# A two-layer conv-attention trunk on one core: partial sums of the last weight matrix placed beside another stage, stores issued later, pools that wait tile by tile

## The chip, the cores and the metric

The kernel runs on 1 core of one Trainium2 chip. The metric is the device time of one execution in microseconds (us), lower is better. The five engines are called PE (TensorE, with PEld for its weight loads), DVE (VectorE), ACT (ScalarE), POOL (GpSimd) and SP (SyncE). SP does no arithmetic here: it issues every DMA of the kernel, one after the other, and a DMA that has to wait for a semaphore holds all that stand behind it.

## What is computed

Sequence 1024, width 1024, two layers in fp32. Layer 0 is a conformer convolution and a gated feed-forward (FFN, 2816 hidden). Layer 1 is causal differential attention (8 heads) and a second FFN:

```python
h = rms_norm(x, norm_g[l, 0]) * (1.0 + sc_m) + sh_m
y = conformer_conv(...) if l < N_CONV_LAYERS else diff_attention(h, k_shared, v_shared, ...)
x = x + g_m * rms_norm(y, norm_g[l, 1])
h = rms_norm(x, norm_g[l, 2]) * (1.0 + sc_f) + sh_f
y = conv_ffn(h, ffn_w_in[l], ffn_dw[l], ffn_dwb[l], ffn_w_out[l])
x = x + g_f * rms_norm(y, norm_g[l, 3])
```

with `conv_ffn(h) = (silu(g) * v) @ w_out`, where `g, v = split(causal_dwconv(h @ w_in))`.

## The kernel before, in words

Every matrix product is made exact enough by splitting each fp32 operand into a high and a low part: ACT copies the high part (`whi`, `wh`), POOL or DVE subtracts (`wlo`, `wl`), and PE makes three products for each. Weights come as 512 KB `raw` tiles (three buffers) through `wsplit`; `plan['pool']` says which share of the low parts POOL makes. The 1024 tokens go through the first part of the program (pools of `front`) in two halves of 512:

1. convolution of both halves, FFN of layer 0 on the first half, `qkv(0)`: Q, K, V of the first half (about 860 to 990 us);
2. FFN of layer 0 on the second half (`ffn(0, 1, ...)`), with three generators handed out beside its 60 steps by `interleave`: attention of the first half (`attn`, 48 steps), rows of the modulation (`gate_row`, `mod_scale`, `mod_col`), and `front_sums` (about 990 to 1445 us);
3. `wo_pre`, the residual and `wo_half` of the first half (to about 1565 us);
4. `qkv(1)`: Q, K, V of the second half, with the transposes of the first half's output beside V (to about 1706 us). Results go to DRAM (`qd`, `kd`, `vd`, `hfd`); `front.close()` ends the pools.
5. attention of the second half (about 1706 to 1965 us), with pools `back`, `ab` and four in PSUM. Its 37 steps (32 tiles of 128 queries, 4 to a head, and a tail) are written out by hand under `tc.manual_schedule()`: the instructions of each engine, SP's DMAs too, keep the order of the text. Beside each step stand a unit of the last FFN's first two products (`First.unit`, `one_more`) and two ticks of `sums_s`.
6. `wo` of the second half (pools `op`, `bp`), and the last FFN on all 1024 tokens, whose two products are made with 7 block products instead of 8.

Outside stage 5 the order on an engine is the framework's: it takes the text's order as a priority and places an instruction as soon as what it needs is there and, for a tile, a buffer is free.

The 7-product form needs sums of weight blocks. `sums_t(j, u, v)` (11 of them, line 933) loads two 512 KB tiles of `w_out`, makes four subtractions of 128x512 on POOL (line 940) and stores both tiles to `ftd` (lines 942, 943), which stage 6 reads. `sums_s(q, x, y, s)` (22 of them, line 945) does the like for `w_in`: two loads, four POOL operations (lines 951 to 957) and three stores to `sxd`, `syd`, `s1d` (lines 958 to 960), 1.25 MB. `front_sums` (line 962) makes all 11 `sums_t` and then `sums_s` for q = 10 to 21 in stage 2, with two `p4` buffers and one `p2`; q = 0 to 9 are made in stage 5.

In stage 5 a step's DMAs stand in this order: `load_kq` of the next head (lines 1141 to 1144, at step 1 of a head), `load_v` (line 1151, at step 0), the store of an attention result `o` (line 1227, every second step), the store of a unit's result `X` to `fdx` (line 1110), the next `rx` (line 1072), and the ticks of `sums_s`. Each store is issued where its data is made. The tag `q` of `back` (13 buffers of 4 KB) holds K, Q, `rx`, `ry` and `X`.

```python
def unit(self, mk):
    ...
    A.copy(self.x[:, (1 - i) * 512:(2 - i) * 512], ps)
    if i == 1:
        dma(out=fdx[q], in_=self.x)
```

Of the kernel before, what the change touches and what calls it, by code (L numbers as in the profile page):

```python
# [12 lines left out]
F32 = mybir.dt.float32  # L13
# [59 lines left out]
NWS, NSS, NQ, NHS = 12, 6, 13, 40  # L73
LA = 5
LAT = 4
QS = 10


# [28 lines left out]
def drain(g):  # L107
    for _ in g:
        pass
# [3 lines left out]
def trunk(ctx: ExitStack, tc: tile.TileContext, x, mw, cols, grow, w1, w2, wk, wv, wq, wo, win, wout, relb, onehot, lamr, out):  # L113
# [18 lines left out]
    def nm(s):  # L132
        uid[0] += 1
        return f"{s}_{uid[0]}"
# [10 lines left out]
    def pbank(pool, tag, name=None):  # L145
        return pool.tile([P, 512], F32, tag=tag, name=nm(name or "P" + tag))
# [556 lines left out]
    def qkv(half, hq, hkv, also_q=iter(()), also_v=iter(())):  # L703
        def stored(ps, scale, dst):
            hl = big.tile([P, 1024], F32R, tag="yf", bufs=4, name=nm("hl"))
            hi, lo = hl[:, 0:512], hl[:, 512:1024]
            if scale is None:
                A.copy(hi, ps)
                V.tensor_tensor(out=lo, in0=ps, in1=hi.bitcast(F32), op=ALU.subtract)
            else:  # L710
                A.activation(hi, ps, AF.Copy, scale=scale)
                V.scalar_tensor_tensor(out=lo, in0=ps, scalar=scale, in1=hi.bitcast(F32), op0=ALU.mult, op1=ALU.subtract)
            dma(out=dst, in_=hl.bitcast(F32).rearrange("p (l t) -> p l t", l=2))

        for h in range(NH):
            next(also_q, None)
            ps = pbank(pu, "u")
            featmm(ps, [wsplit(wq[h])], hq)
            stored(ps, 0.125, qd[h][half])
        for h in range(NH):  # L720
            ps = pbank(pu, "u")
            featmm(ps, [wsplit(wk[h])], hkv)
            stored(ps, None, kd[h][:, :, half * 512:(half + 1) * 512])

        def evac(t, nh, ps):
            sl = slice(nh * 512, (nh + 1) * 512)
            stored(ps, None, vd[half][t][:, :, sl])
        for nh in range(2):
            for _ in tokmm(hkv, lambda nh, pr: wv[nh, pr], nh, evac):
                next(also_v, None)  # L730
        drain(also_v)

    def two_heads(xn):

# [195 lines left out]

        return t.rearrange("p (k two j) -> p two k j", two=2, j=P)

    def sums_t(j, u, v):

        dma(out=u, in_=wout[1, 0, j])
        dma(out=v, in_=wout[1, 1, j])
        yield
        u0, u1, v0, v1 = u[:, 0:512], u[:, 512:1024], v[:, 0:512], v[:, 512:1024]
        for o, a, b in ((u0, v0, u0), (v0, v1, v0), (v1, v1, u0), (u1, u1, v1)):
            G.tensor_tensor(out=o, in0=a, in1=b, op=ALU.subtract)  # L940
            yield
        dma(out=ftd[j][0], in_=u)
        dma(out=ftd[j][1], in_=v)

    def sums_s(q, x, y, s):

        dma(out=y, in_=win[1, q + FC])
        yield
        (x0, x1), (y0, y1) = [[blocks(t)[:, i] for i in range(2)] for t in (x, y)]
        s_ = s.rearrange("p (k j) -> p k j", j=P)  # L950
        G.tensor_tensor(out=s_, in0=y0, in1=y1, op=ALU.add)
        yield
        G.tensor_tensor(out=y0, in0=x0, in1=y0, op=ALU.subtract)
        yield
        G.tensor_tensor(out=x0, in0=s_, in1=x0, op=ALU.subtract)
        yield
        G.tensor_tensor(out=x1, in0=x1, in1=x0, op=ALU.subtract)
        dma(out=sxd[q], in_=x)
        dma(out=syd[q], in_=y)
        dma(out=s1d[q], in_=s)  # L960
        yield

    def front_sums():
        def p4():
            return pre_.tile([P, 1024], F32, tag="p4", bufs=2, name=nm("p4"))
        for j in range(FC // 2):
            yield from sums_t(j, p4(), p4())
        for q in range(QS, FC):
            x = p4()
            dma(out=x, in_=win[1, q])  # L970
            yield from sums_s(q, x, p4(), pre_.tile([P, 512], F32, tag="p2", bufs=1, name=nm("p2")))

    pre_ = front.enter_context(tc.tile_pool(name="pre", bufs=1))
    gd_m1, gd_f1 = [dr.tile([1, D], F32, name=f"gdrow{n}") for n in range(2)]
# [4 lines left out]
    f = ffn(0, 1, hB, yB, gn_f0, ssB)  # L979
    interleave(itertools.islice(f, 60), (attn(at, 0, ssqA), NAT, 0, AE),  # L980
               (chain(gate_row(1, 2, 1, gn_m1, gd_m1), mod_scale(1, 4, 2, s_f1), mod_col(1, 3, sh_f1),
                       gate_row(1, 5, 3, None, gd_f1)), 32, 0, 60), (front_sums(), 5 * (FC // 2) + 6 * (FC - QS), 0, 60))
    ynA = wo_norm(ssqA)
    actA = []
    alongside(f, wo_pre(0, ynA, gpair, actA))
    xnB = residual(yB, ssB, 1, lambda t: xd[0][t], lambda t: xd[1][t])
    trB, hqB, hkvB = two_heads(xnB)
    xnA = wo_half(0, actA, gn_m1, trB)
    hA = []
    hfd = [dr.tile([P, D], F32, name=f"hfd{j}") for j in range(4)]  # L990
    qkv(1, hqB, hkvB, also_v=transposing(xnA, [hA], (hpair, s_f1, sh_f1), keep=hfd))
    front.close()


    back = ctx.enter_context(tc.tile_pool(name="back", bufs=1))
    att = ExitStack()
    ab = att.enter_context(tc.tile_pool(name="ab", bufs=1))
    psc = att.enter_context(tc.tile_pool(name="psc", bufs=2, space=PSUM))
    ptr = att.enter_context(tc.tile_pool(name="ptr", bufs=1, space=PSUM))
    pav = att.enter_context(tc.tile_pool(name="pav", bufs=1, space=PSUM))  # L1000
    pf = att.enter_context(tc.tile_pool(name="pf", bufs=1, space=PSUM))
    opool, bpool = [None], [None]

    def b2k(name="s"):
# [2 lines left out]
    def b4k(name="q", dt=F32):  # L1007
        return back.tile([P, 1024], dt, tag="q", bufs=NQ, name=nm(name))
# [56 lines left out]
    class First:  # L1065
# [20 lines left out]
        def sums(self, q):  # L1086

            x = self.raws.pop(q)
            if q < QS:
                yield from sums_s(q, x, b4k("ry"), b2k("S"))  # L1090

        def unit(self, mk):

            q, i = divmod(self.u, 2)
            self.u += 1
            if q >= FC:
                return
            if i == 0:
                self.ps, self.x = mk(), b4k("X")
            hi, lo = self.pairs.pop((q, i))  # L1100
            ps = self.ps
            for j in range(4):
                ah, al = H[1 + i][j]
                w, v = hi[:, j * P:(j + 1) * P], lo[:, j * P:(j + 1) * P]
                T.matmul(ps, lhsT=w, rhs=ah, start=(i == 0 and j == 0), stop=False, skip_group_check=True)
                T.matmul(ps, lhsT=w, rhs=al, start=False, stop=False, skip_group_check=True)
                T.matmul(ps, lhsT=v, rhs=ah, start=False, stop=(j == 3), skip_group_check=True)
            A.copy(self.x[:, (1 - i) * 512:(2 - i) * 512], ps)
            if i == 1:
                dma(out=fdx[q], in_=self.x)  # L1110

    first = First()
    bg = []

    def tick(n=1):
        for _ in range(n):
# [98 lines left out]
    def values(h, pr):  # L1215

        ah, al = AV[pr]
        nkb = NT + 2 * pr + 2
        po = pav.tile([P, 512], F32, tag="av", name=nm("Pav"))
        Vh = VV[h]  # L1220
        for kb in range(nkb):
            T.matmul(po[:, 0:256], lhsT=Vh[0][:, kb, :], rhs=ah[:, kb, :], start=(kb == 0), stop=False, skip_group_check=True)
            T.matmul(po[:, 0:256], lhsT=Vh[0][:, kb, :], rhs=al[:, kb, :], start=False, stop=False, skip_group_check=True)
            T.matmul(po[:, 0:256], lhsT=Vh[1][:, kb, :], rhs=ah[:, kb, :], start=False, stop=(kb == nkb - 1), skip_group_check=True)
        o = b2k("o")
        A.copy(o[:, 0:256], po[:, 0:256])
        dma(out=od[h][1][:, pr * 256:(pr + 1) * 256], in_=o[:, 0:256])
        sq = b2k("sq")
        A.activation(sq[:, 0:256], po[:, 0:256], AF.Square)
        return po, sq  # L1230
# [35 lines left out]
    for i in range(NTL + 5):  # L1266
        if i % NT == 1 and i // NT + 1 < NH:
            load_kq(i // NT + 1)
        if i % NT == 0 and i < NTL:
            load_v(i // NT)  # L1270
        if i < NTL:
            maxima(i)
        if 0 <= i - 2 < NTL:
            turned(i - 2)
        if i < NTL:
            exps(i)
        if i + 1 < NTL:
            scores(i + 1, 0)
            scores(i + 1, 1)
        t = i - 3  # L1280
        if i % 2 == 0 and 0 <= t < NTL:
            pairs[t] = values(t // NT, (t % NT) // 2)
        if t - 1 in pairs:
            squares(*pairs[t - 1])
        more(i)
        if 0 <= i - 2 < NTL:
            turned_lo(i - 2)
        if 0 <= i - 1 < NTL:
            difference(i - 1)
        if t - 1 in pairs:  # L1290
            V.tensor_copy(ss[:, t - 2:t], pairs.pop(t - 1)[0][:, 256:258])


    v = bsm(NTL)
    V.scalar_tensor_tensor(out=v, in0=r0, scalar=2.0 * HD * EPS, in1=r0, op0=ALU.mult, op1=ALU.mult)
# [1 line left out]
    yn = bnewton(v, NTL)  # L1297
    inorder.__exit__(None, None, None)
    att.close()
    opool[0] = ctx.enter_context(tc.tile_pool(name="op", bufs=1))  # L1300
    bpool[0] = ctx.enter_context(tc.tile_pool(name="bp", bufs=1, space=PSUM))


    bplan["pool"] = 0.4
# [395 lines left out]
```

## Time and profile before

| | us |
|---|---|
| median of 3 runs (lowest to highest) | 2668.21 (2660.86 to 2669.43) |
| the profiled execution, its own time | 2669.41 |
| its span, first to last instruction | 2667.6 |
| PE busy in the span | 2400.3 (90%) |
| DVE busy | 1924.2 (72%) |
| POOL busy | 962.3 (36%) |
| DMA moved | 499.54 MB, 187 GB/s in the mean |

Line numbers with L are those of the kernel before. Idle time in front of an instruction is put down to what ended it. A matmul's duration overlaps the next one's, so that busy PE time is a share of time in which some matmul was running. PEclk is the granted clock of TensorE as a share of its full speed, DMA share the mean busy share of the 16 DMA engines.

### The profile page before, as it was taken

How to read it: one execution, taken by the hardware profiler on the slowest of the kernel's cores; microseconds unless marked ns; L12 is line 12 of the kernel's file. 1: busy time of each engine (PE TensorE's matmuls, PEld its weight loads, DVE VectorE, ACT ScalarE, POOL GpSimd, SP SyncE). 2: the span in 40 equal slices, each digit the busy share in tenths (PEclk: the TensorE clock that was granted, in tenths of full speed). 3: DMA queues.
4: the chain of work that ended last, by engine and by line, in shares of the span. 5: the costliest groups of instructions: out<-in, count | busy, mean ns of one | idle time of the engine just before them, and what ended most of it. 6: DMA issues, size and time to landing. Idle time of an engine off the chain costs nothing. (4 is left out here: it accounts for less than half of the span.)

```text
span 2667.6 us, 30514 instructions
## 1 busy us (share of the span) xinstructions
PE 2400.3 (90%) x10346; PEld 1887.5 (71%) x10346; DVE 1924.2 (72%) x3072; ACT 1137.7 (43%) x1871; POOL 962.3 (36%) x578
## 2 busy tenths in 40 slices
PE   5998889999988988898889999787899899999997
PEld 4666667777766766776767777576777677777875
DVE  6998689999778346757757771366664799997556
ACT  4434244332444235535534352254543544444543
POOL 2234334444534453554544323142242211213221
PEclk9999999999999998999999999898999999999999
DMA  7123643434345776677776356688863645555656
GB/s 274 56 64 111 216 163 103 156 121 128 103 140 186 268 270 201 223 252 231 237 234 231 126 184 195 193 242 239 222 230 119 234 174 186 190 197 193 198 184 218
DMA packets 204811, 499.54 MB, mean 187 GB/s; under 512 B 24432, under 2 KB 64752, under 8 KB 204656
## 3 DMA queue, kind: packets, MB, share of 16 engines
q1 hardware_dynamic: 204656, 497.60, 57.2%
q8 instruction: 82, 1.34, 0.2%
q14 instruction: 73, 0.60, 0.1%
HBM read 375.61 MB, written 121.91 MB: 187 GB/s over the span
## 5 line engine op out<-in xcount | busy, mean ns | idle before, releaser
L208 POOL TENSOR_TENSOR wlo<-raw,whi 128x1024 fp32r<-128x1024 f32 x204 | 509.3, 2498 | 758.3 <-ACT whi L207 738.1
L207 ACT CAST whi<-raw 128x1024 fp32r<-128x1024 f32 x234 | 244.9, 1047 | 466.9 <-issue 249.2
L228 PE MATMUL Pu<-hT,whi 128*128 128x512 f32 x832 | 341.6, 411 | 27.1 <-DVE tap L426 16.7
L230 PE MATMUL Pu<-hT,wlo 128*128 128x512 f32 x832 | 338.7, 407 | 12.7 <-POOL wlo L208 10.9
L229 PE MATMUL Pu<-hT,whi 128*128 128x512 f32 x832 | 337.7, 406 | 3.3 <-DVE hT L308 3.2
L493 DVE SCALAR_TENSOR_TENSOR Pcv<-cu,sv,Pcv 128x512 f32<-128x512 f32 x432 | 299.8, 747 | 3.5 <-PE Pcv L488 2.6
L243 PE MATMUL Py<-whi,gT 128*128 128x512 f32 x608 | 247.6, 408 | 15.6 <-DVE yf L447 9.5
L244 PE MATMUL Py<-wlo,gT 128*128 128x512 f32 x608 | 244.2, 402 | 7.7 <-POOL wlo L208 7.7
L245 PE MATMUL Py<-whi,gT 128*128 128x512 f32 x608 | 243.1, 400 | 0.5 <-DVE gT L185 0.5
L228 PEld LDWEIGHTS Pu<-hT,whi 128*128 128x128 f32 x832 | 161.3, 194 | 71.0 <-issue 20.4
L230 PEld LDWEIGHTS Pu<-hT,wlo 128*128 128x128 f32 x832 | 161.3, 194 | 55.2 <-POOL wlo L208 14.6
L363 DVE CUSTOM_DVE_ANT_0 mraw<-mraw,crow 128x1024 f32<-128x1024 f32 x96 | 149.1, 1554 | 68.0 <-DMA mraw<-in_mw_dram 67.9
L229 PEld LDWEIGHTS Pu<-hT,whi 128*128 128x128 f32 x832 | 161.4, 194 | 41.3 <-DVE hT L308 4.5
L243 PEld LDWEIGHTS Py<-whi,gT 128*128 128x128 f32 x608 | 116.8, 192 | 45.3 <-issue 14.5
L244 PEld LDWEIGHTS Py<-wlo,gT 128*128 128x128 f32 x608 | 116.9, 192 | 36.0 <-POOL wlo L208 9.9
L245 PEld LDWEIGHTS Py<-whi,gT 128*128 128x128 f32 x608 | 116.4, 191 | 28.3 <-DVE gT L185 1.0
L1045 DVE TENSOR_TENSOR op<-raw,op 128x512 fp32r<-128x512 f32 x115 | 91.8, 823 | 60.9 <-ACT op L1044 53.6
L1044 ACT CAST op<-raw 128x512 fp32r<-128x512 f32 x154 | 93.1, 621 | 85.4 <-DMA raw<-fad 27.9
L1589 PE MATMUL Py<-op,op 128*128 128x512 f32 x308 | 121.6, 395 | 6.7 <-ACT op L1044 5.8
L1590 PE MATMUL Py<-op,op 128*128 128x512 f32 x308 | 122.2, 397 | 4.3 <-POOL op L1045 3.5
L1591 PE MATMUL Py<-op,op 128*128 128x512 f32 x308 | 121.0, 393 | 0.0
L1045 POOL TENSOR_TENSOR wl<-rx,wh 128x512 fp32r<-128x512 f32 x44 | 58.1, 1338 | 169.8 <-ACT wh L1044 169.5
(327 smaller groups left out, 5715.3 us busy)
## 6 DMA issues: line engine op xcount, KB each, us to landing
mraw<-in_mw_dram SPq DMA_DIRECT2D x96, 512.0 KB, 5.0
raw<-in_win_dram SPq DMA_DIRECT2D x88, 512.0 KB, 4.1
raw<-in_w_dram SPq DMA_DIRECT2D x48, 512.0 KB, 3.6
raw<-in_wout_dram SPq DMA_DIRECT2D x44, 512.0 KB, 4.0
raw<-fad SPq DMA_DIRECT2D x77, 256.0 KB, 3.8
K<-kd SPq DMA_DIRECT2D x48, 256.0 KB, 7.2
V<-vd SPq DMA_DIRECT2D x48, 256.0 KB, 6.0
p<-in_win_dram SPq DMA_DIRECT2D x24, 512.0 KB, 5.4
```

What stands on the lines that cost most here:

```text
L207: A.copy(hi, raw)
L208: e.tensor_tensor(out=lo, in0=raw, in1=hi.bitcast(F32), op=ALU.subtract)
L228: T.matmul(ps, lhsT=a, rhs=ah, start=(k == 0), stop=False)
L229: T.matmul(ps, lhsT=a, rhs=al, start=False, stop=False)
L230: T.matmul(ps, lhsT=b, rhs=ah, start=False, stop=(k == KC - 1))
L243: T.matmul(ps[t], lhsT=a, rhs=rh, start=(f == 0), stop=False)
L244: T.matmul(ps[t], lhsT=a, rhs=rl, start=False, stop=False)
L245: T.matmul(ps[t], lhsT=b, rhs=rh, start=False, stop=(f == n - 1))
L363: V.tensor_tensor_reduce(out=raw, in0=raw, in1=crow, scale=1.0, scalar=0.0, op0=ALU.mult, op1=ALU.add, accum_out=r[:, k:k + 1])
L493: V.scalar_tensor_tensor(out=ps, in0=u[:, j:j + 512], scalar=col("dw", j * 8 + c), in1=ps, op0=ALU.mult, op1=ALU.add)
L1045: e.tensor_tensor(out=lo, in0=src, in1=hi.bitcast(F32), op=ALU.subtract)
L1590: T.matmul(ps[t], lhsT=a, rhs=bl, start=False, stop=False, **more_)
```

## The change

`front_sums` now takes the lists of j and q. In stage 2 only q = 10 to 21 are handed out; the 11 `sums_t` become a generator `ft`, stepped beside `qkv(1)`: three steps ahead of each of the 8 Q and the 8 K products and two at each V step, then drained. Both use four `p4` buffers and two `p2` (`NPRE = 4`), and hold their stores back until the loads of the next pair have been written down. In the hand-ordered stage 5, `store` puts a DMA into a list instead of issuing it, and `stores(i)` issues those that are due, after `load_kq` and `load_v` of step i and ahead of its arithmetic: `o` and `fdx` one step later, the three of `sums_s` two steps later. Before the loop starts and after it ends, a store is issued at once. The pools `back`, `ab`, `psc`, `ptr`, `pav`, `pf`, `op` and `bp` are opened with `reuse_waits="tile"`: the first writer of a tile waits for the earlier tiles whose place it takes, not for the release of all of the earlier pools.

```diff
+NPRE = 4
@@ qkv
         for h in range(NH):
+            if half == 1:
+                next(also_q, None)
             ps = pbank(pu, "u")
             featmm(ps, [wsplit(wk[h])], hkv)
@@
-        drain(also_v)
+        if half == 0:
+            drain(also_v)
@@ sums_t, sums_s
-        dma(out=ftd[j][0], in_=u)
-        dma(out=ftd[j][1], in_=v)
+        st(ftd[j][0], u)
+        st(ftd[j][1], v)
...
-        dma(out=sxd[q], in_=x)
-        dma(out=syd[q], in_=y)
-        dma(out=s1d[q], in_=s)
+        st(sxd[q], x)
+        st(syd[q], y)
+        st(s1d[q], s)
@@
-    def front_sums():
+    def front_sums(js, qs):
         def p4():
-            return pre_.tile([P, 1024], F32, tag="p4", bufs=2, name=nm("p4"))
-        for j in range(FC // 2):
-            yield from sums_t(j, p4(), p4())
-        for q in range(QS, FC):
+            return pre_.tile([P, 1024], F32, tag="p4", bufs=NPRE, name=nm("p4"))
+        held = []
+        def st(out, in_):
+            held.append((out, in_))
+        def flush(n):
+            while len(held) > n:
+                o, i = held.pop(0)
+                dma(out=o, in_=i)
+        for j in js:
+            g = sums_t(j, p4(), p4(), st)
+            next(g)
+            flush(0)
+            yield
+            yield from g
+        for q in qs:
...
+        flush(0)
@@ stage 2
-  (front_sums(), 5 * (FC // 2) + 6 * (FC - QS), 0, 60))
+  (front_sums((), range(QS, FC)), 6 * (FC - QS), 0, 60))
@@ stage 4
+    ft = front_sums(range(FC // 2), ())
...
+    def beside(g, n):
+        while True:
+            for _ in range(n):
+                next(ft, None)
+            yield next(g, None)
-    qkv(1, hqB, hkvB, also_v=transposing(xnA, ...))
+    qkv(1, hqB, hkvB, beside(iter(()), 3), beside(transposing(xnA, ...), 2))
+    drain(ft)
     front.close()
-    back = ctx.enter_context(tc.tile_pool(name="back", bufs=1))
+    back = ctx.enter_context(tc.tile_pool(name="back", bufs=1, reuse_waits="tile"))
@@ stage 5 (ab, psc, ptr, pav, pf, op and bp likewise)
-                yield from sums_s(q, x, b4k("ry"), b2k("S"))
+                yield from sums_s(q, x, b4k("ry"), b2k("S"), lambda o, i: store(o, i, 2))
-                dma(out=fdx[q], in_=self.x)
+                store(fdx[q], self.x)
-        dma(out=od[h][1][:, pr * 256:(pr + 1) * 256], in_=o[:, 0:256])
+        store(od[h][1][:, pr * 256:(pr + 1) * 256], o[:, 0:256])
+    def store(out, in_, steps=1):
+        if now[0] is None:
+            dma(out=out, in_=in_)
+        else:
+            waiting.append((now[0] + steps, out, in_))
+    def stores(step):
+        now[0] = step
+        due = [w for w in waiting if step is None or w[0] <= step]
+        waiting[:] = [w for w in waiting if step is not None and w[0] > step]
+        for _, o, i in due:
+            dma(out=o, in_=i)
@@ the loop
             load_v(i // NT)
+        stores(i)
...
+    stores(None)
```

## Rows read from the trace of the kernel before

**Rows 1.** Windows by stage: us, busy (instructions) of each engine, PEclk, DMA share, GB/s

```profile
860.00:1015.00 155.00, 142.12 (x601) 111.34 (x600) 75.41 (x122) 49.11 (x68) 77.20 (x39) 0.97 0.79 274
1015.00:1445.00 430.00, 372.31 (x1659) 297.88 (x1658) 297.16 (x672) 207.09 (x351) 206.22 (x137) 0.93 0.71 229
1565.00:1706.00 141.00, 138.81 (x613) 111.42 (x612) 56.37 (x91) 51.13 (x76) 39.92 (x18) 1.00 0.56 187
1706.00:1723.00 17.00, 2.49 (x12) 1.86 (x11) 3.58 (x7) 2.07 (x4) 2.00 (x6) 0.61 0.82 235
1723.00:1965.00 242.00, 199.00 (x1100) 169.12 (x1099) 149.82 (x271) 122.14 (x232) 81.22 (x60) 0.91 0.81 229
1965.00:2109.00 144.00, 128.45 (x521) 96.90 (x519) 86.15 (x148) 67.69 (x128) 44.92 (x32) 0.96 0.53 182
```

**Rows 2.** Waits of PE in 1723 to 1965: us in total, times, longest

```profile
PE Psc L1162 <- DMA K<-kd: 19.8, 6, 4.2
...
PE Psc L1162 <- DVE p L1193: 5.5, 2, 2.8
```

**Rows 3.** Waits of SP's queue in 1735 to 2000, and its timeline at head 4

```profile
SPq L1110 <- ACT X L1108: 72.1, 11, 12.0
SPq L958 <- POOL rx L957: 27.3, 5, 9.0
SPq L1227 <- ACT a L1204: 10.3, 5, 2.5
...
1817.15 0.32 SPq L1110 DMA_DIRECT2D fdx<-X  x1
...
1824.11 0.45 SPq L1141 DMA_DIRECT2D Q<-qd  x1
...
1828.72 0.59 SPq L1142 DMA_DIRECT2D K<-kd  x1
```

**Rows 4.** SP's timeline from stage 4 to stage 5, and PE's first scores

```profile
1708.74 1.68 SPq L713 DMA_DIRECT2D vd<-hl  x2
1714.38 0.50 SPq L1141 DMA_DIRECT2D Q<-qd  x1
...
1721.94 1.62 PE L1162 MATMUL Psc<-K,Q 128*128 128x512 f32 x4 [14.51 <-DMA K<-kd]
1726.56 0.77 PE L1162 MATMUL Psc<-K,Q 128*128 128x512 f32 x1 [3.00 <-DMA K<-kd]
```

**Rows 5.** Lines 680 and 940: durations in ns, first and last start in us

```profile
L680 POOL MEMSET rbt<- x1: 104/104/104, 1.8 to 1.8; 128x8 f32 x1
...
L940 POOL TENSOR_TENSOR p<-p,p x33: 1261/1294/2292, 836.5 to 1154.4; 128x512 f32<-128x512 f32 x33
```

**Rows 6.** The first matmuls of stage 2, line 228, in 990 to 1020

```profile
L228 PE MATMUL Pu<-hT,whi x33: 392/396/628, 990.5 to 1018.3; 128*128 128x512 f32 x33
```

**Rows 7.** Waits of SP's queue and of PE in stage 2, 1015 to 1445

```profile
SPq L942 <- POOL p L940: 35.6, 4, 9.8
SPq L958 <- POOL p L957: 34.2, 10, 7.6
...
PE Ptr L843 <- DVE p L826: 18.4, 11, 5.8
```

**Rows 8.** POOL by line in stage 2 (count | busy us, mean ns), and DVE's low parts (line 208)

```profile
L940 POOL TENSOR_TENSOR p<-p,p 128x512 f32<-128x512 f32 x17 | 26.6, 1565 | 41.1 <-DMA p<-in_wout_dram 36.5 <-issue 3.7
...
L940 POOL TENSOR_TENSOR p<-p 128x512 f32<-128x512 f32 x5 | 8.1, 1627 | 0.4
...
L208 DVE TENSOR_TENSOR wlo<-raw,whi x16: 1219/1226/3016, 1031.3 to 1442.6; 128x1024 fp32r<-128x1024 f32 x16
```

**Rows 9.** Windows: the highest DMA rate of stage 4, and two heads of stage 5

```profile
1580.00:1600.00 20.00, 19.66 (x84) 15.37 (x83) 12.44 (x24) 8.17 (x13) 6.07 (x4) 1.00 0.91 323
1797.00:1824.00 27.00, 19.36 (x106) 16.76 (x105) 14.04 (x25) 11.35 (x23) 6.99 (x5) 0.81 0.81 224
1851.00:1878.00 27.00, 22.80 (x133) 19.41 (x132) 18.19 (x35) 14.41 (x29) 8.18 (x6) 0.94 0.85 233
```

**Rows 10.** POOL's timeline in `qkv(0)`: four subtractions ahead of two low parts

```profile
914.77 1.29 POOL L940 TENSOR_TENSOR p<-p,p 128x512 f32<-128x512 f32 x1 [0.83 <-DMA p<-in_wout_dram]
916.14 1.29 POOL L940 TENSOR_TENSOR p<-p 128x512 f32<-128x512 f32 x1
917.51 2.66 POOL L940 TENSOR_TENSOR p<-p,p 128x512 f32<-128x512 f32 x2
920.13 5.75 POOL L208 TENSOR_TENSOR wlo<-raw,whi 128x1024 fp32r<-128x1024 f32 x2
```

**Rows 11.** POOL by line in stage 4, 1565 to 1706

```profile
L208 POOL TENSOR_TENSOR wlo<-raw,whi 128x1024 fp32r<-128x1024 f32 x16 | 38.7, 2419 | 87.4 <-ACT whi L207 87.3
```

**Rows 12.** The page's groups: the cast of a weight's high part on ACT

```profile
L207 ACT CAST whi<-raw 128x1024 fp32r<-128x1024 f32 x234 | 244.9, 1047 | 466.9 <-issue 249.2
```

More of the change, by code (lines that the diff above doesn't have):

```diff
@@ L931, in blocks, with sums_t @@
         return t.rearrange("p (k two j) -> p two k j", two=2, j=P)
-    def sums_t(j, u, v):
+    def sums_t(j, u, v, st):
         dma(out=u, in_=wout[1, 0, j])
@@ L941, in sums_t, with sums_s @@
             yield
-        dma(out=ftd[j][0], in_=u)
-        dma(out=ftd[j][1], in_=v)
-    def sums_s(q, x, y, s):
+        st(ftd[j][0], u)
+        st(ftd[j][1], v)
+    def sums_s(q, x, y, s, st):
         dma(out=y, in_=win[1, q + FC])
@@ L957, in sums_s @@
         G.tensor_tensor(out=x1, in0=x1, in1=x0, op=ALU.subtract)
-        dma(out=sxd[q], in_=x)
-        dma(out=syd[q], in_=y)
-        dma(out=s1d[q], in_=s)
+        st(sxd[q], x)
+        st(syd[q], y)
+        st(s1d[q], s)
         yield
-    def front_sums():
+    def front_sums(js, qs):
         def p4():
-            return pre_.tile([P, 1024], F32, tag="p4", bufs=2, name=nm("p4"))
-        for j in range(FC // 2):
-            yield from sums_t(j, p4(), p4())
-        for q in range(QS, FC):
+            return pre_.tile([P, 1024], F32, tag="p4", bufs=NPRE, name=nm("p4"))
[13 more added lines that the diff above has]
+        for q in qs:
             x = p4()
             dma(out=x, in_=win[1, q])
-            yield from sums_s(q, x, p4(), pre_.tile([P, 512], F32, tag="p2", bufs=1, name=nm("p2")))
+            g = sums_s(q, x, p4(), pre_.tile([P, 512], F32, tag="p2", bufs=NPRE // 2, name=nm("p2")), st)
+            next(g)
+            flush(0)
+            yield
+            yield from g
+        flush(0)
     pre_ = front.enter_context(tc.tile_pool(name="pre", bufs=1))
@@ L981, in trunk @@
                (chain(gate_row(1, 2, 1, gn_m1, gd_m1), mod_scale(1, 4, 2, s_f1), mod_col(1, 3, sh_f1),
-                       gate_row(1, 5, 3, None, gd_f1)), 32, 0, 60), (front_sums(), 5 * (FC // 2) + 6 * (FC - QS), 0, 60))
+                       gate_row(1, 5, 3, None, gd_f1)), 32, 0, 60), (front_sums((), range(QS, FC)), 6 * (FC - QS), 0, 60))
     ynA = wo_norm(ssqA)
@@ L990, in trunk @@
     hfd = [dr.tile([P, D], F32, name=f"hfd{j}") for j in range(4)]
-    qkv(1, hqB, hkvB, also_v=transposing(xnA, [hA], (hpair, s_f1, sh_f1), keep=hfd))
+    def beside(g, n):
[3 more added lines that the diff above has]
+            yield next(g, None)
+    qkv(1, hqB, hkvB, beside(iter(()), 3), beside(transposing(xnA, [hA], (hpair, s_f1, sh_f1), keep=hfd), 2))
+    drain(ft)
     front.close()
-    back = ctx.enter_context(tc.tile_pool(name="back", bufs=1))
+    back = ctx.enter_context(tc.tile_pool(name="back", bufs=1, reuse_waits="tile"))
     att = ExitStack()
[L997 to L1001, printed above, removed]
+    ab = att.enter_context(tc.tile_pool(name="ab", bufs=1, reuse_waits="tile"))
+    psc = att.enter_context(tc.tile_pool(name="psc", bufs=2, space=PSUM, reuse_waits="tile"))
+    ptr = att.enter_context(tc.tile_pool(name="ptr", bufs=1, space=PSUM, reuse_waits="tile"))
+    pav = att.enter_context(tc.tile_pool(name="pav", bufs=1, space=PSUM, reuse_waits="tile"))
+    pf = att.enter_context(tc.tile_pool(name="pf", bufs=1, space=PSUM, reuse_waits="tile"))
     opool, bpool = [None], [None]
@@ L1109, in unit @@
             if i == 1:
-                dma(out=fdx[q], in_=self.x)
+                store(fdx[q], self.x)
     first = First()
     bg = []
+    waiting = []
+    now = [None]
+    def store(out, in_, steps=1):
[9 more added lines that the diff above has]
+            dma(out=o, in_=i)
     def tick(n=1):
@@ L1299, in trunk @@
     att.close()
-    opool[0] = ctx.enter_context(tc.tile_pool(name="op", bufs=1))
-    bpool[0] = ctx.enter_context(tc.tile_pool(name="bp", bufs=1, space=PSUM))
+    opool[0] = ctx.enter_context(tc.tile_pool(name="op", bufs=1, reuse_waits="tile"))
+    bpool[0] = ctx.enter_context(tc.tile_pool(name="bp", bufs=1, space=PSUM, reuse_waits="tile"))
     bplan["pool"] = 0.4
```

## The prediction

> **What bounds the kernel now.** I read the windows by stage first, then who waits for whom, then SP's timeline where PE waits for a DMA. In the windows the reader is to see that PE is the engine that the stages share, but not equally: `qkv(1)` is full of matmuls (138.8 of 141 us, clock 1.00), while 58 us are idle in stage 2 (372.3 of 430), 14.5 of 17 at the change of pools, and 43 in the second half's attention (199.0 of 242, clock 0.91) [rows 1]. The rest of the program, some 1500 us, is touched by no line of the diff but the pools `op` and `bp`, so it keeps its time.
>
> In the attention of the second half PE's largest wait is for K: six times, 19.8 us, and 5.5 us more at the same matmul for a DVE result [rows 2]. SP's queue shows why K is late. SP stands 72.1 us in front of the store `fdx`, 27.3 in front of `sxd`, 10.3 in front of `od` [rows 3]. In head 4 `fdx` goes out at 1817.15; then follow `rx`, `ry`, V and an `od` store that also waits; the eight Q and K loads go from 1824.1 to 1828.7 [rows 3]. It is a ring: the scores wait for K, the next unit stands behind the scores on PE, its `fdx` behind the unit, and the next K behind `fdx`. At the change of pools the last `vd` store is issued by 1710.4, the first Q load only at 1714.4, and PE stands 14.5 and then 3.0 us for K [rows 4].
>
> In stage 2 SP stands 35.6 us in front of `ftd` stores and 34.2 in front of `sxd` stores, but PE's largest wait, 18.4 us, is for DVE [rows 7]; how much of the 58 us the sums cause, no row says.
>
> **Part 1: where the sums go.** The text moves 11 pairs (22 loads and 22 stores of 512 KB, 44 POOL subtractions) beside `qkv(1)`. Outside stage 5, however, the order is the framework's, and the trace shows how far it pulls work forward: the memset of line 680, written after the first half's FFN, runs at 1.8 us, and the first `ftd` subtraction runs at 836.5 [rows 5], 154 us before the first matmul of the FFN that it is written beside, 990.5 [rows 6]. It starts when a `p4` buffer is there. So I expect `sums_s` for q = 10 to 21 to start at about 840 in its place, and `sums_t` to follow as soon as buffers come free, still inside stage 2, not beside `qkv(1)`: the two kinds change places, and four buffers put two groups in flight where there was one. The work is the same; it comes earlier and denser.
>
> That costs in `qkv(0)`, where POOL's four operations of a group already stand ahead of two low parts [rows 10] and DMA is at 0.79 [rows 1], and gives back late in stage 2. Ends: PE's whole idle time in 860 to 1015 once more, 155 - 142 = 13 us lost; or stage 2's idle 58 us in the share of `sums_t` there, 22 of its 22 + 48 POOL operations, 18 us gained. Work that only changes its order is nearest to nothing: I take the middle, **3 us gained**.
>
> **Part 2: the change of pools.** K and Q of head 0 are the first tiles of `back`, which by the order of opening take the place of `crow` and of the `raw` tiles; those are read for the last time some us before V's last matmul. With waits by tile the loads need not stand behind the `vd` stores, and the scores' first PSUM banks were those of Q and K's products, long free. The lower end is that the loads are still placed behind the stores and only the landing is not waited for: 1714.4 - 1710.4 = 4 us [rows 4]. A loss is excluded as the new waits are a part of the old. The upper end is both waits, 14.5 + 3.0 = 17.5 us. I cannot see which place each tile takes; V of head 0 still waits for `vd`, but is needed four steps later. I take **10 us**, about half way.
>
> **Part 3: stores one and two steps later.** Now `load_kq` at step 1 of a head stands behind `stores` of step 0, whose `fdx` is that of the last step, and no longer behind the `od` store of step 0. V goes out ahead of `fdx`. From head 4: K could follow `fdx` and a `rx` at once, 1817.5 in place of 1824.1, over 6 us earlier, more than the longest of the six waits, 4.2 us. So the 19.8 us should go. What holds the later stores' tiles: with K and Q of two heads (8), two `rx`, one `ry` and one `X`, I count 12 of the 13 buffers at `load_kq`, so nothing waits for a held store; that excludes a loss from buffers. What is late next is DVE's difference, 5.5 us at the same matmul, and the DMA: a head without a K wait has DMA busy 0.85 of 27 us, 23 us [rows 9], so at most 4 us of a head can go. Ends: nothing (DVE's chain takes K's place each time) and 19.8 + 5.5 = 25 us. I take **16 us**, near the sum of the K waits, as part of each is likely to come back as a wait for DVE. The clock needs no term of its own: it was 0.81 in the head with two K waits, 0.94 in one with none [rows 9], and what that is worth lies inside the bounds.
>
> **Part 4: `op` and `bp`.** The first `wo` work needs `yn`, which stands behind the whole attention, so waits by tile find little: 1965 to 2109 idles 16 us in all [rows 1], mostly later on. **1 us**, between nothing and 4 (a quarter of it).
>
> Sum: 3 + 10 + 16 + 1 = 30 us. The profiled execution took 2669.4 us (span 2667.6, 1.8 around it), 1.2 above the median of 2668.2, so 2639.4 against its own time; I predict **2640 us**.
>
> **The rivals.**
>
> *Only the hand-ordered parts fall short* (chance 0.16). The loads stay behind the `vd` stores (4 us) and DVE takes K's place in all but two of the heads (5 us); the sums give nothing: 2669.4 - 9 = 2660. For it: heads with no K wait are no shorter than those with one, about 27 us [rows 9]. Against it: a wait for DVE of nearly K's size may be the same late K, seen through the DVE semaphore.
>
> *The sums do leave stage 2* (0.14), as the text says, and `qkv(1)` hides them. Then stage 2 gains the 18 us in place of 3: 2669.4 - 45 = 2624. For it: POOL is busy for only 38.7 us of low parts in `qkv(1)` [rows 11], and 44 x 1.3 = 57 more fit into 141. Against it: [rows 5]. The row that bears on its size: DVE's subtraction takes 1226 ns at the median but up to 3016 in stage 2, where POOL runs beside it [rows 8]. The Trainium skill, "SBUF — State Buffer", section "Who interferes with whom", says that a DVE instruction with two SBUF inputs and a POOL instruction that reads SBUF exclude each other, the second standing until the first is done. The trace agrees, as the 1.8 us more are less than one POOL low part. By that rule the 22 subtractions of [rows 8] (26.6 + 8.1 us) could each hold DVE, up to 35 us of it, and the time could fall to 2669 - 27 - 35 = 2607; I give that only a small part of this rival's chance, as POOL stands in other gaps too.
>
> *The sums beside `qkv(1)` make it slower* (0.09). It needs that they really stand there. PE uses a weight in 141 / 24 = 5.9 us; cast and low part take 1.0 + 2.4 [rows 11, 12], so 2.4 us are spare, and four subtractions in a row, 5.2 us [rows 10], ahead of a low part cost 2.8 us in each of 11 pairs: 31 us. DMA would carry 187 x 141 = 26.4 MB and 23.1 more; at the highest rate of that stage, 323 GB/s [rows 9], that takes 153 us, 12 more than the stage has. With parts 2 to 4 at 27 us it ends at 2669.4 - 27 + 43 = 2685. It decides from 2.5 us lost per pair. By the Trainium skill's page "DMA: Bandwidth & Descriptors" (Specifications: about 358 GB/s of HBM for one core) the same 49.5 MB would need an estimated 138 us and just fit; no run here shows that rate.
>
> *Nothing moves* (0.05): the waits by tile are not drawn otherwise, and what SP stops waiting for it waits for elsewhere: 2668.
>
> **How the numbers follow.** My own case has 0.56 and reaches from 30 + 15 + 9 (all upper ends but a part of them) to 30 - 22 us of gain, about 2614 to 2662. The range takes in the rivals at 2624, 2660 and 2668 and leaves out the slower one and the last of both tails: **2608 to 2669**. A measurement of this kernel tells about 0.3%, 8 us, from no change, so faster means under 2660. Faster: 0.53 of my case, 0.14, and 0.09 of the short-fall, 0.76. Within 0.3%: the rest of the short-fall, *nothing moves* and a little of my case, 0.14. Slower: 0.10.
>
> **What would show it.** Right: `ftd` subtractions on POOL end well before 1565 and start after the last `sxd` store of stage 2; the first scores follow V's last matmul by a few us; SP's waits in front of `fdx` and `sxd` fall and PE's wait for K in heads 2 to 8 is near nothing, with heads of about 25 us. Wrong: line 940 between 1565 and 1706; a gap of 14 us still before the first scores; heads still of 27 us with PE waiting for DVE in K's place; or `qkv(1)` longer than 141 us with PE waiting for POOL.

## The result, and the profile after

The changed kernel took 2631.36 us (median of 4 runs, 2625.70 to 2635.43) beside 2664.61 for the kernel before on the same chip (2660.86 to 2669.43): ratio 0.9873, 95% interval 0.9845 to 0.9901. Its profiled execution took 2630.61 us, with a span of 2628.8, 38.8 below that of before. The forecast was 2640 in 2608 to 2669. The total fits, its terms don't, as the stages show.

The windows by stage of the changed kernel, as in [rows 1] (us, busy time of PE, PEld, DVE, ACT, POOL with instructions, PEclk, DMA share, GB/s):

```profile
1015.00:1424.00 409.00, 374.55 (x1713) 301.44 (x1712) 288.75 (x689) 210.18 (x359) 192.65 (x136) 0.97 0.75 242
...
1545.00:1686.00 141.00, 139.22 (x616) 111.77 (x614) 58.34 (x92) 52.22 (x77) 42.04 (x24) 1.00 0.57 187
1686.00:1698.00 12.00, 0.46 (x1) 0.49 (x2) 1.31 (x4) 0.09 (x1) 0.00 (x0) 0.58 1.03 295
1698.00:1924.00 226.00, 193.98 (x1102) 170.08 (x1101) 159.06 (x271) 121.74 (x232) 83.58 (x60) 0.92 0.86 250
```

`qkv(1)` is what it was, full at 141 us. Stage 2 is shorter, with 34 us of idle PE in place of 58 and PEclk at 0.97 in place of 0.93, and so is the attention of the second half, with 32 idle in place of 43. Stage borders, read from the starts of single instructions in both traces, put it in numbers. Each comes from one execution; the first of them, read in the four profiled executions whose first three stages are those of the changed kernel, lies between 1545.2 and 1548.4.

| border (us) | before | after | gain in the stage |
|---|---|---|---|
| last copy of `wo_half`, end of stages 1 to 3 (L907, now L911) | 1566.1 | 1545.2 | 20.9 |
| last `hfd` store, end of `qkv(1)` (L305, L306) | 1708.3 | 1686.1 | 1.3 |
| first scores (L1162, L1210) | 1721.9 | 1697.5 | 2.2 |
| last sums of squares of the attention (L1235, L1283) | 1965.2 | 1924.2 | 16.6 |
| first gate product of the FFN (L1524, L1575) | 2113.6 | 2076.3 | -3.7 |
| last product (L1589, L1640) | 2655.1 | 2616.4 | 1.4 |

The sums' subtractions, by line (ns min/median/max, first and last start in us): those of the last matrix (line 944, 940 in [rows 5]) stand in stage 2, far ahead of `qkv(1)`, where the text has them:

```profile
L944 POOL TENSOR_TENSOR p<-p,p x33: 1261/1292/2127, 1262.9 to 1431.4; 128x512 f32<-128x512 f32 x33
...
L961 POOL TENSOR_TENSOR p<-p x12: 1259/1294/2161, 840.9 to 1206.7; 128x512 f32<-128x512 f32 x12
```

SP's waits in 860 to 1440 in front of the sums' stores (line 979). Before, SP stood 102.0 us there at lines 942, 943 and 958 to 960, most of it in [rows 7]; now 20.8, all at `ftd`:

```profile
SPq L979 <- POOL p L944: 18.3, 5, 5.0
...
SPq L979 <- DMA p<-in_wout_dram: 2.5, 1, 2.5
```

SP does not stand less in all, 388.7 us before and 378.3 after; it now stands in front of weight loads, for a `raw` buffer to come free, 176.3 us where it was 105.1. The largest such wait before, then after:

```profile
SPq L192 <- POOL wlo L208: 72.9, 26, 13.1
```

```profile
SPq L193 <- POOL wlo L209: 115.8, 41, 13.0
```

From 860 us to the last copy of `wo_half` PE's idle time fell from 75.5 to 58.8 us and its busy time from 630.6 to 626.4. Nearly all of the idle time has a name, and what fell are the waits for DVE results, 54.2 to 38.2 us together.

The change of pools, SP's timeline and PE's first scores, as in [rows 4]. The first Q load now follows the last `vd` store at once (1688.23, 1688.28), but is still behind it. PE's second gap stays too, now with no cause named:

```profile
1686.54 1.69 SPq L714 DMA_DIRECT2D vd<-hl  x2
1688.28 1.27 SPq L1189 DMA_DIRECT2D Q<-qd  x1
...
1697.54 1.62 PE L1210 MATMUL Psc<-K,Q 128*128 128x512 f32 x4 [12.31 <-DMA K<-kd]
1702.46 2.05 PE L1210 MATMUL Psc<-K,Q 128*128 128x512 f32 x5 [3.30 <-issue]
```

PE's waits in the attention, 1698 to 1924. Of seven waits for K the first is left; the transposes' wait for DVE, 13.2 us before, is 27.2:

```profile
PE Ptr L1251 <- DVE p L1241: 27.2, 9, 4.6
PE Psc L1210 <- DMA K<-kd: 12.3, 1, 12.3
```

And SP at a head, as in [rows 3]: `fdx` goes out, and the next head's Q follows 0.4 us later, where it took 7.0 before:

```profile
1777.88 0.33 SPq L1161 DMA_DIRECT2D fdx<-X  x1
1778.26 0.45 SPq L1189 DMA_DIRECT2D Q<-qd  x1
```

### The profile page after: what moved, and what is told of

The parts are those of the page before. It is cut to its first block, busy times and chain, and to the rows that moved or that the text cites. A ratio compares the mean times of both kernels' runs of the same rounds, so it can differ in the third digit from the quotient of the medians.

```text
span 2628.8 us, 30492 instructions
## 1 busy us (share of the span) xinstructions
PE 2392.7 (91%) x10346; PEld 1888.8 (72%) x10346; DVE 1925.4 (73%) x3072; ACT 1135.1 (43%) x1869; POOL 948.9 (36%) x578
## 5 line engine op out<-in xcount | busy, mean ns | idle before, releaser
L364 DVE CUSTOM_DVE_ANT_0 mraw<-mraw,crow 128x1024 f32<-128x1024 f32 x96 | 138.2, 1442 | 60.5 <-DMA mraw<-in_mw_dram 60.5
L1640 PE MATMUL Py<-op,op 128*128 128x512 f32 x308 | 121.7, 395 | 6.7 <-ACT op L1075 4.8
```

The costliest lines, as they stand in the source:

```text
L1640: T.matmul(ps[t], lhsT=a, rhs=bh, start=(p in OPEN and j == 0), stop=False, **more_)
```

## The experiments

Diffs are against the changed kernel; "last copy" is the last copy of `wo_half`, the end of the first three stages.

### The hand-ordered stage: stores at once

```diff
 def store(out, in_, steps=1):
-    if now[0] is None:
-        dma(out=out, in_=in_)
-    else:
-        waiting.append((now[0] + steps, out, in_))
+    dma(out=out, in_=in_)
```

> The changed kernel, but in the second half's attention every store goes out where its data is made, as before. Theory: the held stores are what took the wait for K away, so the stretch from first to last scores goes from the changed kernel's 200 us back to some 218, the wait for K comes back with about 20 us, and the time is about 2648 us. Rival: the waits by tile did it; then the stretch stays at 200 and the time at 2631 to 2634.

2643.56 us, ratio to before 0.9927 (0.9907 to 0.9946), nearer to the theory than to the rival. The last copy is at 1548.4, the attention takes 239.9 us from the first scores to the last squares where the changed kernel takes 226.7: 13.2 us. PE's waits in 1701 to 1941 bring the K waits back, six with 19.3 us beside the first:

```profile
PE Psc L1207 <- DMA K<-kd: 31.6, 7, 12.3
PE Ptr L1248 <- DVE p L1238: 16.6, 13, 3.3
```

So the held stores are what removed them, and DVE takes back 10.6 of the 19.3 us (27.2 in place of 16.6). The 13.2 us are 10.7 of idle PE (42.8 to 32.1) and 2.5 of shorter busy time.

### Waits by pool

```diff
-    back = ctx.enter_context(tc.tile_pool(name="back", bufs=1, reuse_waits="tile"))
+    back = ctx.enter_context(tc.tile_pool(name="back", bufs=1))
```

and likewise for the seven other pools.

> The changed kernel with all pools waiting for whole earlier pools. Theory: the waits by tile are worth only what the change of pools shows, 2 to 4 us, as the first Q load is still issued behind the last store of V: 2633 to 2636 us, and the first scores come some 14 us after the last hfd store in place of 11. Rival: they are worth the 10 us that were forecast, 2641 us.

2628.38 us, ratio 0.9869 (0.9847 to 0.9890): no difference from the changed kernel that can be told, and below what either expectation had; the first scores, 13.7 us behind the last `hfd` store in place of 11.4, are the theory's. Its SP and PE at the change of pools:

```profile
1687.58 1.69 SPq L714 DMA_DIRECT2D vd<-hl  x2
1693.24 0.50 SPq L1189 DMA_DIRECT2D Q<-qd  x1
...
1700.89 1.62 PE L1210 MATMUL Psc<-K,Q 128*128 128x512 f32 x4 [14.62 <-DMA K<-kd]
```

The 4 us before the first Q load are back, but only 2.3 of them reach PE (14.62 and 12.31). The rest of `reuse_waits` shows nowhere beyond what kernels with waits by tile show among themselves: last squares to first gate product takes 151.5 us here and 152.1 in the changed kernel, first scores to last squares 228.7 and 226.7 (226.4 to 228.8 in ten kernels with both waits by tile and held stores).

### The front: order, buffers and held stores

Three things changed there together. Five kernels undo one or two, one undoes all; the new order with two buffers and held stores was not run. The edits: "old order" hands both kinds of sums out in stage 2, the last matrix's first; "two" is `NPRE = 2`; "at once" issues the store where the data is made.

```diff
-NPRE = 4
+NPRE = 2
...
-            held.append((out, in_))
+            dma(out=out, in_=in_)
...
-  (front_sums((), range(QS, FC)), 6 * (FC - QS), 0, 60))
+  (front_sums(range(FC // 2), range(QS, FC)), 5 * (FC // 2) + 6 * (FC - QS), 0, 60))
...
-    ft = front_sums(range(FC // 2), ())
+    ft = iter(())
```

All undone:

> The changed kernel with the first part wholly as before: order of the sums, two buffers, stores at once; the held stores of the second half's attention and the waits by tile stay. Theory: the first part's share of the gain is the 22 us that the last copy of the squares came earlier, less some 4 that later stages gave back: 2650 to 2654 us, with the last copy at about 1470. Rival: the earlier end of stage 2 is run to run variation of a few us, and the time is 2635 to 2640.

New order, four buffers, stores at once:

> The changed kernel, but the stores of the sums in the first part are written down where their data is made; four buffers and the new order of the two kinds of sums stay. Theory: SP standing in front of these stores is what stage 2 lost, so most of its 20 us gain goes: the last copy of the squares at about 1465 in place of 1448 us, the time at 2646 to 2651. Rival: four buffers or the order gave it; then the last copy stays at about 1448 to 1452 and the time at 2631 to 2636.

New order, two buffers, stores at once:

> The front keeps the new order (sums of the input weights first, those of the last matrix handed out beside Q, K, V of the second half) but has two buffers and one as before, and issues its stores where the data is made; the hand-ordered stage is the changed one. The front undone altogether gave 2649.9 us, with the new order and four buffers but stores at once 2641.2, the changed kernel 2631.4. Theory (order gives nothing, the buffers give the 9 us between the first two): 2646 to 2654, last squares copy of the first half's attention at 1466 to 1472. Rival (the order gives the 9 us, the buffers alone nothing): 2637 to 2644, that copy at 1459 to 1465.

Old order, four buffers, held:

> Both kinds of sums are handed out in stage 2 again, the sums of the last matrix first as in the kernel before; four buffers, held stores, and all of the hand-ordered stage stay as in the changed kernel. Theory (the front's gain comes from the held stores and the added buffers, and the place in the text gives nothing because the sums run in stage 2 either way): 2627 to 2636 us, the last squares copy of the first half's attention at 1446 to 1452 us as in the changed kernel (1447.9). Rival (the late place is what counts, since it makes the sums of the last matrix wait for every load of stage 2): 2643 to 2652 us, that copy at 1460 to 1470.

Old order, four buffers, at once:

> The old order of the sums in stage 2, four buffers and two, stores issued where the data is made; the hand-ordered stage as changed. With two buffers and one this was 2649.9 us, with held stores as well 2621.5. Theory (buffers and held stores each give a part of the 28 us, about 10 of it the held stores as in the new order): 2628 to 2636 us, last squares copy of the first half's attention at 1449 to 1455. Rival (the buffers give nothing as long as the stores stand at the head of SP's queue): 2645 to 2652, that copy at 1465 to 1470.

Old order, two buffers, held:

> The old order of the sums in stage 2, with two buffers and one, but held stores; the hand-ordered stage as changed. Theory (with two buffers the next pair's loads need the held stores to be done, so nothing can be held and the store goes out as before): 2645 to 2652 us, last squares copy of the first half's attention at 1465 to 1470. Rival (the held store alone frees SP's queue, whatever the buffers): 2622 to 2635, that copy below 1455.

The changed kernel again:

> The changed kernel once more, beside the three that follow. With both kinds of sums in stage 2, the last matrix's first, and all else as changed, the time was 2621.5 us; the changed kernel gave 2631.4. Theory (the new order costs the changed kernel about 10 us, as its subtractions crowd the last 170 us of stage 2 and PE waits 15.3 us there and before for POOL's low parts, 3.6 us with the old order): 2627 to 2635 us, 7 or more above the old order with four buffers and held stores. Rival (the two differ by chance of the run): within 3 us of that kernel.

Measured, with SP's time in front of the sums' stores in 860 to 1440:

| order, buffers, stores | time, us | ratio to before (95%) | last copy | SP at the stores |
|---|---|---|---|---|
| old, two, at once | 2649.92 | 0.9941 (0.9924 to 0.9958) | 1565.6 | 99.6 |
| old, two, held | 2641.79 | 0.9909 (0.9888 to 0.9931) | 1563.9 | 98.8 |
| old, four, at once | 2639.38 | 0.9887 (0.9867 to 0.9907) | 1553.9 | 92.4 |
| old, four, held | 2621.49 | 0.9830 (0.9797 to 0.9862) | 1538.0 | 8.6 |
| new, two, at once | 2639.16 | 0.9906 (0.9875 to 0.9938) | 1552.9 | 120.4 |
| new, four, at once | 2641.23 | 0.9914 (0.9891 to 0.9938) | 1558.8 | 87.3 |
| new, four, held (changed) | 2631.36 | 0.9873 (0.9845 to 0.9901) | 1545.2 | 20.8 |
| the same, again | 2626.68 | 0.9840 (0.9817 to 0.9864) | 1546.6 | 20.9 |

With all undone the last copy is where it was before, 1565.6 and 1566.1: the whole of the front's 20 us comes from these three things. Four buffers with held stores bring 27.6 us of the last copy in the old order. One without the other is less: in the old order four buffers alone bring 11.7 us of the last copy and 10.5 of time, held stores alone 1.7 and 8.1, both together 27.6 and 28.4. The last copy is that of the profiled execution; with old order, two buffers and held stores this was the longest of six (2651.40, the median 2641.79), with new order, two buffers and stores at once the shortest of five (2633.96, the median 2639.16), so for these two the time is the better measure. Held stores with two buffers leave SP where it stood, and the last line shows why: the next pair's loads wait for the stores to land. SP's waits there, old order and two buffers, held:

```profile
SPq L979 <- POOL p L961: 42.2, 10, 8.0
SPq L979 <- POOL p L944: 33.8, 8, 5.7
SPq L979 <- POOL p L957: 12.9, 4, 4.7
...
SPq L939 <- DMA ftd<-p: 9.5, 2, 4.9
```

Old order and four buffers, at once:

```profile
SPq L974 <- POOL p L961: 41.8, 7, 9.4
SPq L974 <- POOL p L944: 24.0, 6, 6.4
```

Old order and four buffers, held:

```profile
SPq L979 <- POOL p L961: 8.1, 1, 8.1
SPq L979 <- DMA p<-in_win_dram: 0.5, 1, 0.5
```

With four buffers, holding the stores takes SP away from them (92.4 to 8.6, 87.3 to 20.8) and brings 15.9 and 13.6 us of the last copy. What the buffers bring alone, and what the new order brings with two, does not go with SP's time at the stores (99.6 to 92.4, and up to 120.4). How either reaches DVE, for which PE then waits less, no row shows.

The expectations named the last copy of the squares; the table goes by that of `wo_half`, since in the old order with four buffers and stores at once the first came at 1436.6 and the second only at 1553.9: the attention had run ahead of the FFN. Of the expectations, the one for all undone held; the second and the fifth kernel fell between theory and rival, the third came out in time as the rival had it, the fourth below both. For the sixth the time fell between theory and rival (median 2641.79, 2638.42 to 2651.40), while SP's waits are the theory's. The seventh, 2626.68, is 5.2 us above the old order with four buffers and held stores: neither the 7 or more of the theory nor within the rival's 3.

The order has two signs. With two buffers and stores at once the new one is 12.7 us ahead at the last copy and 10.8 in time; with the other two parts in place it is 7.2 behind, and 5 to 10 in time (2631.36 and 2626.68 beside 2621.49; 2626.68 beside 2616.95 for the old order with one more store held, below, on the same chip). The intervals of the ratios overlap in both cases, so the size of either sign is loose. The text's place beside `qkv(1)` does not move the sums there, but puts them last: `ftd` subtractions start at 1262.9, 56 us after the last start of line 961, and all stand in the last 170 us of stage 2; in the old order all sums are over at about 1395. PE's waits for POOL's low part at line 231 in 860 to 1440, changed kernel, then old order with four buffers, held:

```profile
PE Pu L231 <- POOL wlo L209: 15.3, 3, 6.5
```

```profile
PE Pu L231 <- POOL wlo L209: 3.6, 3, 1.3
```

The second run of the changed kernel has 15.1. The difference, 11.7 us, would be enough, but it is not what PE loses in all: its idle time from 860 us to the last copy is 58.8 us beside 54.3, 4.5 more. No run tested it by itself. Why the new order is better with two buffers, although SP stands longer there, is open.

### The sums really beside `qkv(1)`

```diff
+            u, v = p4(), p4()
+            if j < 2:
+                for o in (u, v):
+                    G.tensor_copy(o[0:1, 0:1], late[0][0:1, 0:1])
-            g = sums_t(j, p4(), p4(), st)
+            g = sums_t(j, u, v, st)
...
     xnA = wo_half(0, actA, gn_m1, trB)
+    late.append(xnA[0])
```

> The changed kernel with eight copies of one element on POOL, from the first half's output into the first four tiles of the last matrix's sums, so that those sums cannot start before Q, K, V of the second half: the 44 subtractions then really stand beside the 24 matrix products there. This is the prediction's third rival made to happen. By that rival stage 4 grows by up to 43 us (31 of them low parts held behind subtractions, 12 the DMA), to 2650 to 2675 us in all. By the second rival stage 4 hides them and stage 2, from 1262.9 us on without 44 subtractions and 23.1 MB, gets shorter by a further 5 to 18 us: 2613 to 2627. My theory: stage 2 gains 5 to 10 and stage 4 loses 10 to 25: 2634 to 2650.

The edit makes four such copies, not eight. 2656.71 us, ratio 0.9964 (0.9944 to 0.9984), in the range of the prediction's third rival and above the theory's. The last copy is at 1524.5: the first three stages gain a further 20.7 us. But from there to the last `hfd` store it takes 193.2 us in place of 140.9. Windows of that stage:

```profile
1524.00:1717.00 193.00, 149.14 (x618) 116.12 (x616) 64.73 (x92) 52.76 (x78) 102.09 (x72) 0.89 0.73 256
...
1560.00:1600.00 40.00, 9.69 (x46) 6.75 (x45) 1.38 (x2) 4.35 (x6) 26.43 (x22) 0.65 0.83 291
1600.00:1640.00 40.00, 30.68 (x107) 23.08 (x108) 15.05 (x12) 7.39 (x9) 26.88 (x17) 0.84 0.82 292
```

PE is idle for 30 of 40 us. In the whole stage it idles 44 us in place of 2, and its busy time is 10 us longer (149.1 for 139.2) with PEclk at 0.89 in place of 1.00. Its waits in 1524 to 1729:

```profile
PE Pu L229 <- ACT whi L208: 33.3, 3, 29.3
PE Pu L231 <- POOL wlo L209: 6.2, 6, 1.7
```

And why the high part is late, in SP's timeline and ACT's:

```profile
1552.13 0.44 SPq L193 DMA_DIRECT2D raw<-in_wq_dram  x1
1555.97 0.33 SPq L939 DMA_DIRECT2D p<-in_wout_dram  x1
...
1566.67 5.58 SPq L981 DMA_DIRECT2D ftd<-p  x3
...
1590.06 0.80 SPq L981 DMA_DIRECT2D ftd<-p  x2
1590.92 1.04 SPq L193 DMA_DIRECT2D raw<-in_wq_dram  x1
...
1597.52 1.04 ACT L208 CAST whi<-raw 128x1024 fp32r<-128x1024 f32 x1 [28.95 <-DMA raw<-in_wq_dram]
```

Between two weight loads, 38.8 us apart, SP issued ten loads of sums and eight stores of them, several of which it waited for. `qkv(1)` loses by the order of SP's queue: PE's waits for low parts from POOL are only 7.9 us (6.2 and 1.7). POOL has a part in it by way of that queue, as SP stood 16.3 of the 38.8 us in front of `ftd` stores for POOL's subtractions. The stage moved 193 x 256 = 49.4 MB, which at [rows 9]'s 323 GB/s is 153 us; it took 193. The Trainium skill's "DMA: Bandwidth & Descriptors" (Specifications) has about 358 GB/s, which would make it an estimated 138 us. No 20 us of this kernel's stage show that rate, the highest is 334 (1590 to 1610); the changed kernel has 343 in the same stage (1560 to 1580).

### The attention results of the first half stored later

```diff
-                dma(out=od[h][half][:, pr * 256:(pr + 1) * 256], in_=o)
...
                 def sums(h=h, pr=pr, sq=sq, o=o):
+                    dma(out=od[h][half][:, pr * 256:(pr + 1) * 256], in_=o)
```

with two buffers for `o`. First with the new order:

> The changed kernel, with the store of a result of the first half's attention written down one pair of steps later and two buffers for that result, so that SP need not stand in front of it. In stage 2 SP stands 7.6 us there for the result and 17.7 for the squares behind it. Theory (any store that waits at the head of SP's queue delays the weight loads behind it, and PE in turn): 2622 to 2629 us, stage 2 shorter by 3 to 8 us. Rival (these waits are covered by the three buffers of weights, or the framework places the store where it was): 2629 to 2635, no difference that can be told.

2625.82 us, ratio 0.9848 (0.9816 to 0.9881), last copy 1546.9. The changed kernel's two runs gave 0.9873 and 0.9840, last copy 1545.2 and 1546.6: no difference that can be told. The time lies in the theory's range, but the stage is not shorter by the 3 to 8 us it wanted. Then with the old order:

> The old order of the sums in stage 2, four buffers and held stores, and the store of the first half's attention results one pair later. Theory (the old order is better with these buffers, the later store of the results gives nothing that can be told, as its two profiles showed the same stage 2): 2618 to 2625 us. Rival one (the later store gives 5 us on its own): 2612 to 2617. Rival two (the old order's advantage was chance): 2627 to 2635.

2616.95 us, ratio 0.9805 (0.9784 to 0.9825), last copy 1531.5, beside 2626.68 and 1546.6 for the changed kernel on the same chip. It is the lowest time of the study. That most of it is the old order stands in the table above (0.9830 without the later store); whether the later store adds to it is open: the time is in the range of rival one, which gave it 5 us, and the last copy 6.5 us before that of the table (1538.0).

## Why the prediction was right, and where its terms were wrong

**The bound** held. SP's queue, with a store in front of loads, was the thing to look at, in the attention as argued and, more than argued, in stage 2, where holding the stores gave 13.6 to 15.9 us with four buffers.

**Part 1** was right in place and wrong in size. The sums stayed in stage 2, the kinds changed places, as [rows 5] had it. The failed step is "Work that only changes its order is nearest to nothing: I take the middle, 3 us gained". The front gave 20.9 us in the profile, above the upper end of 18, and 18.6 between the changed kernel and all of the front undone. With all three parts in place it isn't the order that gave it but four buffers together with held stores, 27.6 us in the old order, of which the new order takes 7.2 back. The prediction had [rows 7] before it, SP 35.6 and 34.2 us in front of the sums' stores, applied that reading to stage 5, and set it aside here because PE's largest named wait was for DVE. Just these waits for DVE are what shrank, by 16.0 of the 16.7 us that PE idles less; how a store's place in SP's queue comes to stand behind a wait for DVE, no row shows. The bounds were worked out from POOL's share and idle PE, and neither prices a queue.

**Part 2** was mis-sized: 2.2 us for 10. The lower end describes what happened: loads behind the `vd` stores, the landing not waited for. The first Q load came 3.9 us earlier against `hfd` (2.2 us behind the last one, 6.1 before), and PE got 2.2 of it. That head 0's tiles could be loaded ahead of those stores was read from the pools' order, but they were issued behind them, as the text has them.

**Part 3** was right: 16 us forecast, 16.6 in the profile, of which 13.2 return when stores go out at once. The 19.8 us of [rows 2] hold the 3.00 at 1726.56 that part 2 had as well [rows 4], so the heads' own K waits were 16.8. In heads 2 to 8 they are gone; heads are 25.5 us apart (Q of two heads at 1752.77 and 1778.26). What comes late next is DVE, as named, with 10.6 us. Of the 16.6 us 11.0 are idle PE and 5.6 shorter busy time, for which the prediction took no term.

**Part 4**, 1 us gained, was wrong in sign: the stage behind the attention lost 3.7 us. It isn't the pools' waits (151.5 us with waits by pool), and held stores can't be told from the spread: with stores at once it took 150.8, in the other kernels 151.1 to 154.7. PE's busy time is 2.2 us longer there (133.5 for 131.3) and its idle time 1.5, with PEclk at 0.94 where the kernel before has 0.97 (to 2109, 0.96 in [rows 1]):

```profile
1924.00:2076.00 152.00, 133.69 (x533) 101.22 (x531) 87.28 (x152) 71.34 (x134) 46.32 (x32) 0.94 0.52 178
```

Why the clock was lower there is open.

So 30 us were forecast and 38.7 came in the profiled pair (20.9 + 1.3 + 2.2 + 16.6 - 3.7 + 1.4); by the ratio, 1.27% of 2664.6, it is 34 us. That the total came out near is in part luck: an error of 18 in part 1 and errors of 8 in part 2 and 5 in part 4 have opposite signs.

**The rivals.** *Only the hand-ordered parts fall short* had the change of pools right and the attention wrong. *The sums really leave stage 2* did not happen; made to happen, it gave the first three stages 20.7 us more, but for all 44 subtractions, where its 18 and its 35 us were worked out for 22, so neither size is confirmed. DVE's busy time from 860 us to the last copy fell with it from 452.9 to 430.6 us, for 943 and 944 instructions, as POOL's fell from 300.9 to 240.1. That DVE instructions with two SBUF inputs and POOL instructions that read SBUF hold each other up is the rule of the Trainium skill's "SBUF — State Buffer" ("Who interferes with whom"). The 22.3 us agree with it; how much of the 20.7 they are, no run separates. *Beside `qkv(1)` slower* had the size near (52 us for 43) and the mechanism wrong: it charged low parts held behind subtractions with 31 us, and PE waited 7.9 us for low parts from POOL. *Nothing moves* fell.

## What to carry to other kernels

When one engine issues every DMA, as SP here, read its waits in front of stores first: a store that waited for its data held every load behind it, and PE's waits could go by another name, DVE's in stage 2. Holding a store back until the next loads are written took SP away from the stores only with the buffers that let those loads go (8.6 us there with four, 98.8 with two), so price buffers and held stores as one term. Where a planner sets the order, the place in the text is a priority, not a time: look where moved work will run, and try the old place with the other parts of the change.

## What the runs showed that was not expected

The same order change had both signs, 12.7 us ahead at the last copy with two buffers and stores at once (10.8 in time), 7.2 behind with four and held. The PEclk of the attention was 0.91 before and 0.92 after: two thirds of its 17 us came from idle time, the rest from busy time, where the clock can have a small part. And one program's executions spread by more than the few us in question: the changed kernel gave 2619.54 to 2635.43 in nine, so differences under 5 us were read from stage borders.
